# A decoder block: 1/rms applied behind the products in place of a normalised x, the second weight unit in quarters, ACT's table loaded by a first dummy square

## The chip, the cores and the metric

The kernel runs on one core of one Trainium2 chip. Its time is the device time of one execution in microseconds (us). Three runs of the kernel before gave 914.89, 915.78 and 917.61, median 915.78. A core has five engines with queues of their own, which meet only through semaphores: TensorE (PE, matrix products into PSUM), VectorE (DVE), ScalarE (ACT), GpSimd (POOL) and SyncE (SP, which here only starts DMA transfers). Each executes its instructions in the order in which they stand.

## The reference, cut to what matters

One block over 512 positions with 1024 channels, in float32:

```
h  = rmsnorm(x, g_mix);  z = h @ w_in            # a, gate | q, k | v | two gates
u  = a * sigmoid(gate)                           # GLU
yc = silu(layernorm(conv31(u))) @ w_conv_pw      # depthwise, causal, 31 taps
q, k = rope(q), rope(k);  o = diff_attention(q, k, v)       # 8 heads, two softmaxes each
ya = rmsnorm(o, g_subln) * 0.8 @ w_attn_pw
x  = x + (gate_conv * yc + gate_attn * ya) @ w_out
h2 = rmsnorm(x, g_ffn)
x  = x + (silu(h2 @ w_gate) * (h2 @ w_up)) @ w_down
out = rmsnorm(x, g_final)
```

with `rmsnorm(x, g) = x * rsqrt(mean(x*x) + eps) * g` over the channels. The first rmsnorm is what the change is about: a row's factor 1/rms can be multiplied to x ahead of `w_in` or to the products behind it.

## The kernel before

**Data.** Activations lie transposed, channels on the 128 partitions and the 512 positions along the free axis; x is eight tiles `xt[0..7]`. All weights are cut into units of 128 x 1024 (512 KB) that are used one after the other. Every fp32 factor is split into a high part in the matmul's type fp32r and a low part, the remainder, and a product takes three matmuls of 128x512 (hi by hi, hi by lo, lo by hi). Of a unit, ACT casts the high part (`wh`), and the low part (`wl`) is a subtraction: on DVE for units 0 to 2 and from 64 on, on POOL in two halves for the others (`emit_split`, line 322). `next_unit` (341) starts the loads and splits of later units each time one is taken.

**A chunk** (`chunkA`, 404) takes two units and makes two outputs of 128x512 in PSUM, 48 matmuls in all. With `kouter` both outputs advance together, otherwise the first is done ahead of the second inside each unit. Eight chunks make the inputs of the GLU (i = 0 to 7), then come project_v and the q and k chunks of eight heads, eight chunks of gates, four of w_attn_pw, w_conv_pw and w_out each, and the feed-forward part.

**Start.** Line 433 on loads x tiles and the first unit in quarters, turn by turn, then unit 1 in one piece. `xg` is `xt * g_mix`, split, but not yet divided by the rms. The first three GLU chunks work on `xg`; meanwhile `SumSq` (364) squares the eight tiles on ACT and adds them up on DVE. The task `norm_x` (554) takes over: column sums on PE (`rstd_cols`, 380), the power -1/2 on POOL (`rc`), four diagonal tiles `dg` on DVE, a product that spreads them over the partitions (`bcast_cols`, 390), and the copy `R`, which holds 1/rms of each position on every partition.

**Before, R was used twice.** The GLU outputs of chunks 0 to 2 were multiplied by R behind the products (`evac_glu`, 520): DVE `t = gate * R`, ACT sigmoid, POOL `t * R`, DVE `u = a * t`. In the meantime `renorm` (545) made the normalised x: eight times `xt * g_mix * R` on DVE, split into `hn`, casts on ACT and subtractions on DVE. From chunk 3 on (`SWITCH`) everything used `hn`.

**The order** is fixed when the program is built. A model of the engines' clocks (`Model`, with costs per operation) decides where the work of tasks such as `norm_x`, the softmaxes or `conv_norm` goes between the matmuls. The 31 taps of each channel's convolution (`conv_ops`, 500 on) are filler: DVE gets one whenever the model's DVE clock is behind its PE clock, or waits for something. The convolution's norm (`conv_norm`) can start only when all 8 x 31 taps are done.

**Tail** (1015 to 1034): for each quarter of the positions the sum, a square with accumulation, `ms` by a power on POOL, then `x2 * ms * g_final` on DVE, `x0 * ms` on ACT, and two transfers out.

Of the kernel before, what the change touches and what calls it, by code (L numbers as in the profile page):

```python
# [17 lines left out]
FILL = 0.1  # L18
NCH = 2
NAT = 3  # L20
SWITCH = 3
# [146 lines left out]
def build(nw):  # L168
# [26 lines left out]
    with tile.TileContext(nc) as tc, contextlib.ExitStack() as homes:  # L195
# [3 lines left out]
        with tc.tile_pool(name="cn", bufs=1) as cn, \  # L199
# [5 lines left out]
            def nm(s):  # L205
                uid[0] += 1
                return f"{s}_{uid[0]}"
# [210 lines left out]

            warm = tl("T6", F32R)
            V.memset(f32(warm), 0.0)  # L420
            cold = psum("cv")
            for i in range(10):
                mm(cold, warm[:, 0:P], warm, True, True)
# [11 lines left out]
            raw0 = home["wr"].tile([P, 1024], F32, name=nm("wr"), tag="wr", bufs=3)  # L435
            model.alloc("wr", 3, raw0)
            first = []
            for i in range(4):
                load_x(i)
                w = slice(i * 256, (i + 1) * 256)  # L440
                load(raw0[:, w], w_d[0, :, w])
            wst["dma"] = wst["split"] = 1
            for i in range(4, 6):
                load_x(i)
            emit_dma()
            for i in range(6, 8):
                load_x(i)
            emit_dma()
            lamv = tl("T5")[:, :4 * HD]
            pick = cn.tile([P, 64], F32R, name="pick")  # L450
# [9 lines left out]
            make_identity(nc, ident)  # L460
            load(vec, vec_d)
            ss = SumSq("T3", V)
            hi0 = home["wh"].tile([P, 1024], F32R, name=nm("wh"), tag="wh", bufs=4)
            model.alloc("wh", 4, hi0)
            lo0 = home["wl"].tile([P, 1024], F32R, name=nm("wl"), tag="wl", bufs=4)
            model.alloc("wl", 4, lo0)
            wq.append((hi0, lo0))
            for i in range(8):
                w = slice(i * 256, (i + 1) * 256)
                if i == 0:  # L470
                    V.tensor_copy(hi0[:, w], raw0[:, w])
                xg.append(split_scaled(xt[i], gmix[:, i:i + 1], "T5"))
                if i < 4:
                    if i:
                        S.copy(hi0[:, w], raw0[:, w])
                    V.tensor_tensor(out=lo0[:, w], in0=raw0[:, w], in1=f32(hi0)[:, w], op=ALU.subtract)
                if i == 5:
                    emit_split()
            for i in range(8):
                ss.add(xt[i])  # L480
                if i == 2:
# [5 lines left out]


            R = tl("T6")
            hn = []  # L490
            co = [None] * 8
            csum, done = [], []

# [26 lines left out]
            def evac_glu(i):  # L520
                def f(c, ps):
                    if c == 0:
                        glu["a"] = ps
                        return
                    room("T5", 1)
                    t = tl("T5")
                    u = tl("T2")
                    V.memset(u[:, 0:CW - 1], 0.0)
                    if i < SWITCH:
                        V.tensor_tensor(out=t, in0=ps, in1=R, op=ALU.mult)  # L530
                        S.activation(t, t, AF.Sigmoid)
                        G.tensor_tensor(out=t, in0=t, in1=R, op=ALU.mult)
                    else:
                        S.activation(t, ps, AF.Sigmoid)
                    V.tensor_tensor(out=u[:, CW - 1:CW - 1 + T], in0=glu["a"], in1=t, op=ALU.mult)
                    drop("T5")
                    pend.append([0.0, conv_ops(i, u)])
                return f
# [3 lines left out]
            def hold(c, ps):  # L542
                held.append((c, ps))

            def renorm():
                for i in range(8):
                    yield clk["dve"]
                    V.scalar_tensor_tensor(out=xt[i], in0=xt[i], scalar=gmix[:, i:i + 1], in1=R, op0=ALU.mult, op1=ALU.mult)
                    if i:
                        hn.append(split(xt[i - 1], "T1"))  # L550
                hn.append(split(xt[7], "T1"))
                drop("T4", 8)

            def norm_x():
                yield need(ss.acc) + 1.5
                rc = yield from rstd_cols(ss.acc, 1e-6, "at")
                drop("T3", 8)
                pb = yield from bcast_cols(rc, "at")
# [12 lines left out]
            def when_normed(c, ps):  # L571
                drain_tasks("norm_x")
                second(c, ps)
                if c == 1:
                    spawn(renorm())
# [154 lines left out]
            def project_v(vhl):  # L730
                units = [next_unit(), next_unit()]
                for half in range(2):
                    room("T4", 2)
                    ps = psum("mm")
                    vh, vl = tl("T4", F32R), tl("T4", F32R)
                    for tt in range(2):
                        t = 2 * half + tt
                        sl = slice(tt * 256, (tt + 1) * 256)
                        xs = slice(t * P, (t + 1) * P)
                        for k in range(8):  # L740
                            hi, lo = units[k // 4]
                            yield need(hi, lo, ps)
                            w = slice((k % 4) * 256, (k % 4) * 256 + 256)
                            mm(ps[:, sl], hn[k][0][:, xs], hi[:, w], k == 0, False)
                            mm(ps[:, sl], hn[k][0][:, xs], lo[:, w], False, False)
                            mm(ps[:, sl], hn[k][1][:, xs], hi[:, w], False, k == 7)
                    S.copy(vh, ps)
                    V.tensor_tensor(out=vl, in0=ps, in1=f32(vh), op=ALU.subtract)
                    vhl.append((vh, vl))

            for h in range(NH):
                if h % 2 == 0:
                    vhl = []
                    run(project_v(vhl))
                qk = []
                run(chunkA(hn, [psum("mm"), psum("mm")], lambda c, ps: qk.append(rope(ps))))
                spawn(softmaxes(h, qk))
                spawn(outputs(h, vhl))

# [3 lines left out]
            def evac_gate(i):  # L763
                gs = []
                gates.append(gs)

                def f(c, ps):
                    g = tl("T4")
# [95 lines left out]

            spawn(head_norm())
            for i in range(8):
                run(chunkA(hn, [psum("mm"), psum("mm")], evac_gate(i)))
            drain_tasks("head_norm")
            spawn(conv_norm())

# [115 lines left out]
            for n in range(2):  # L986
# [24 lines left out]
                for t in range(4):  # L1011
# [50 lines left out]
```

## Time and profile before

| | |
|---|---|
| median of the runs | 915.78 us (914.89 to 917.61) |
| the profiled execution | 912.36 us, its span 910.6 us |
| PE | 882.8 us busy, 97%, 4246 matmuls |
| DVE | 573.1 us busy, 63%, 952 instructions |
| ACT | 373.7 us busy, 41% |
| POOL | 264.1 us busy, 29% |
| weights and x by queue q1 | 82.52 MB |

All times in rows are microseconds from the span's start. A row of a timeline gives the start, the duration, the engine, the operation and its tiles; in brackets stands how long the engine had stood idle before, and what ended that. Rows of like instructions that follow each other are put together with a count, so that their duration goes from the first one's start to the last one's end. Neighbours on one engine overlap a little (an instruction starts before the one ahead has written its last), so that distances between starts say more than durations. Since a helper records every operation, nearly all have the same line, and the names of tiles tell them apart: `mm`, `at` and `cv` are PSUM banks, `T` any of the large SBUF tiles, `wr`, `wh`, `wl` a weight unit raw, high and low.

### The profile page before, as it was taken

How to read it: one execution, taken by the hardware profiler on the slowest of the kernel's cores; microseconds unless marked ns; L12 is line 12 of the kernel's file. 1: busy time of each engine (PE TensorE's matmuls, PEld its weight loads, DVE VectorE, ACT ScalarE, POOL GpSimd, SP SyncE). 2: the span in 40 equal slices, each digit the busy share in tenths (PEclk: the TensorE clock that was granted, in tenths of full speed). 3: DMA queues.
4: the chain of work that ended last, by engine and by line, in shares of the span. 5: the costliest groups of instructions: out<-in, count | busy, mean ns of one | idle time of the engine just before them, and what ended most of it. 6: DMA issues, size and time to landing. Idle time of an engine off the chain costs nothing.

```text
span 910.6 us, 11126 instructions
## 1 busy us (share of the span) xinstructions
PE 882.8 (97%) x4246; PEld 730.8 (80%) x4246; DVE 573.1 (63%) x952; ACT 373.7 (41%) x615; POOL 264.1 (29%) x215
## 2 busy tenths in 40 slices
PE   8989999989998999999999999999999999999996
PEld 5768888878886777687888888888888888888886
DVE  6699999898989999957455563343343443422422
ACT  6332336655756874445322343322222222312212
POOL 2654566564736345454100001111111111000000
PEclk9999999999999999999999999999999999999999
DMA  8222222121211222222323441223333222332302
GB/s 278 93 87 100 92 90 74 64 77 47 93 47 46 70 73 72 76 102 92 100 73 133 153 148 51 90 94 107 103 109 98 93 93 92 116 99 87 116 24 93
DMA packets 26150, 85.20 MB, mean 94 GB/s; under 512 B 3040, under 2 KB 3808, under 8 KB 26096
## 3 DMA queue, kind: packets, MB, share of 16 engines
q1 hardware_dynamic: 24944, 82.52, 27.3%
q10 hardware_dynamic: 1152, 1.97, 0.6%
q8 instruction: 33, 0.54, 0.2%
q14 instruction: 21, 0.17, 0.1%
HBM read 82.38 MB, written 2.10 MB: 93 GB/s over the span
## 4 chain that ended last, share of the span: by engine, by line
PE 52%; DVE 0%; issue 0%; POOL 0%; ACT 0%; POOLq 0%
PE mm L141 27%; PE at L141 22%; PE cv L141 4%; DVE dg L141 0%; DVE T L141 0%; POOL rc L141 0%; ACT T L141 0%; POOLq L195 0%; POOL sm L141 0%; DVE fs L141 0%
## 5 line engine op out<-in xcount | busy, mean ns | idle before, releaser
L141 PE MATMUL mm<-T,wh 128*128 128x512 f32 x1360 | 424.9, 393 | 4.4 <-DVE T L141 3.5
L141 PEld LDWEIGHTS mm<-T,wh 128*128 128x128 f32 x1360 | 250.3, 188 | 58.2 <-DVE T L141 4.2
L141 PE MATMUL mm<-T,wl 128*128 128x512 f32 x680 | 265.6, 391 | 0.5 <-DVE wl L141 0.5
L141 POOL TENSOR_TENSOR wl<-wr,wh 128x512 fp32r<-128x512 f32 x122 | 165.9, 1385 | 174.8 <-ACT wh L141 167.5
L141 ACT CAST wh<-wr 128x1024 fp32r<-128x1024 f32 (+1 forms) x148 | 148.7, 1033 | 79.3 <-PE mm L141 38.7
L141 DVE SCALAR_TENSOR_TENSOR cv<-T,vec_sb,cv 128x512 f32<-128x512 f32 x232 | 160.5, 746 | 0.1
L141 POOL TENSOR_TENSOR T<-T,T 128x512 f32<-128x512 f32 x64 | 84.2, 1320 | 242.1 <-DVE T L141 220.7
L141 PE MATMUL at<-T,wh 128*128 128x512 f32 x496 | 154.3, 392 | 0.0
L141 PEld LDWEIGHTS mm<-T,wl 128*128 128x128 f32 x680 | 127.7, 188 | 28.4 <-DVE wl L141 1.0
L141 DVE TENSOR_TENSOR wl<-wr,wh 128x1024 fp32r<-128x1024 f32 (+1 forms) x88 | 101.9, 1186 | 69.7 <-ACT wh L141 69.3
L141 DVE TENSOR_TENSOR T<-T,T 128x512 fp32r<-128x512 f32 (+2 forms) x111 | 88.4, 798 | 58.3 <-ACT T L141 56.1
L141 ACT CAST T<-T 128x512 fp32r<-128x512 f32 (+2 forms) x112 | 67.6, 618 | 135.5 <-POOL T L141 82.2
L141 PEld LDWEIGHTS at<-T,wh 128*128 128x128 f32 x496 | 93.6, 189 | 19.5
L141 DVE TENSOR_TENSOR T<-mm,T 128x512 f32<-128x512 f32 (+1 forms) x76 | 51.7, 682 | 84.9 <-PE mm L141 77.3
L141 PE MATMUL mm<-wh,T 128*128 128x256 f32 (+1 forms) x432 | 100.5, 317 | 0.0
L141 PE MATMUL at<-T,wl 128*128 128x512 f32 x248 | 97.0, 391 | 0.0
L141 ACT ACTIVATE T<-T 128x512 f32<-128x512 f32 (+1 forms) x66 | 40.4, 621 | 123.8 <-DVE T L141 123.7
L141 DVE TENSOR_TENSOR T<-at,T 128x512 f32<-128x512 f32 (+4 forms) x59 | 38.0, 649 | 67.1 <-PE at L141 56.0
L141 ACT ACTIVATE T<-T,sm 128x128 f32<-128x128 f32 (+3 forms) x100 | 56.1, 562 | 58.5 <-DVE sm L141 55.1
L141 PEld LDWEIGHTS mm<-wh,T 128*128 128x128 f32 x432 | 73.0, 190 | 5.4
L141 PE MATMUL mm<-wl,T 128*128 128x256 f32 (+1 forms) x216 | 68.2, 316 | 0.0
L141 PEld LDWEIGHTS at<-T,wl 128*128 128x128 f32 x248 | 46.9, 189 | 9.8
(88 smaller groups left out, 651.9 us busy)
## 6 DMA issues: line engine op xcount, KB each, us to landing
wr<-wall SPq DMA_DIRECT2D x145, 512.0 KB, 3.3
T<-xT SPq DMA_DIRECT2D x16, 256.0 KB, 4.8
out<-T ACTq DMA_DIRECT2D x4, 256.0 KB, 2.8
out<-T SPq DMA_DIRECT2D x4, 256.0 KB, 2.6
wr<-wall SPq DMA_DIRECT2D x4, 128.0 KB, 4.4
T<-cs ACTq DMA_DIRECT2D x2, 256.0 KB, 4.6
T<-gfin SPq DMA_DIRECT2D x2, 256.0 KB, 4.6
T<-mask ACTq DMA_DIRECT2D x1, 256.0 KB, 5.0
```

What stands on the lines that cost most here:

```text
L141: r = f(*args, **kw)
```

## The change

- `xg` is kept for all of `w_in`; `renorm`, `hn` and `SWITCH` are gone, and with them the `kouter` order of chunk 3.
- R enters behind the products: in all eight GLU chunks, in the two rope tables `cs` (once, behind chunk 3), in the gates (a DVE product ahead of each sigmoid), and for v, where positions lie on partitions, by the column factors `rc`, in halves of 256 columns on ACT and DVE.
- Unit 1 is loaded and split in quarters as unit 0 is, beside x4 to x7; unit 2's split stands behind that loop, unit 3's where unit 2's was, behind the third square.
- A square of one column of the zeroed `warm` tile is ACT's first instruction, so that its table is loaded then.
- In the tail `x2 * g_final` comes ahead of the factor `ms`, and for the last quarter half of `x0 * ms` goes from ACT to DVE.

```diff
@@ start
             V.memset(f32(warm), 0.0)
+            S.activation(small(), f32(warm)[:, 0:1], AF.Square)
...
-            for i in range(4):
+            for i in range(8):
                 load_x(i)
-                w = slice(i * 256, (i + 1) * 256)
-                load(raw0[:, w], w_d[0, :, w])
-            wst["dma"] = wst["split"] = 1
-            for i in range(4, 6):
-                load_x(i)
-            emit_dma()
-            for i in range(6, 8):
-                load_x(i)
+                w = slice(i % 4 * 256, i % 4 * 256 + 256)
+                load(raws[i // 4][:, w], w_d[i // 4, :, w])
+            wst["dma"] = wst["split"] = 2
             emit_dma()
...
-                xg.append(split_scaled(xt[i], gmix[:, i:i + 1], "T5"))
-                if i < 4:
-                    if i:
-                        S.copy(hi0[:, w], raw0[:, w])
-                    V.tensor_tensor(out=lo0[:, w], in0=raw0[:, w], in1=f32(hi0)[:, w], op=ALU.subtract)
-                if i == 5:
-                    emit_split()
+                    V.tensor_copy(hi[:, w], raw[:, w])
+                xg.append(split_scaled(xt[i], gmix[:, i:i + 1], "T1"))
+                if i:
+                    S.copy(hi[:, w], raw[:, w])
+                V.tensor_tensor(out=lo[:, w], in0=raw[:, w], in1=f32(hi)[:, w], op=ALU.subtract)
+            emit_split()
             for i in range(8):
                 ss.add(xt[i])
                 if i == 2:
                     emit_split()
@@ evac_glu
-                    if i < SWITCH:
-                        V.tensor_tensor(out=t, in0=ps, in1=R, op=ALU.mult)
-                        S.activation(t, t, AF.Sigmoid)
-                        G.tensor_tensor(out=t, in0=t, in1=R, op=ALU.mult)
-                    else:
-                        S.activation(t, ps, AF.Sigmoid)
+                    V.tensor_tensor(out=t, in0=ps, in1=R, op=ALU.mult)
+                    S.activation(t, t, AF.Sigmoid)
+                    G.tensor_tensor(out=t, in0=t, in1=R, op=ALU.mult)
@@ renorm
-            def renorm():
-                for i in range(8):
-                    yield clk["dve"]
-                    V.scalar_tensor_tensor(out=xt[i], in0=xt[i], scalar=gmix[:, i:i + 1], in1=R, op0=ALU.mult, op1=ALU.mult)
-                    if i:
-                        hn.append(split(xt[i - 1], "T1"))
-                hn.append(split(xt[7], "T1"))
-                drop("T4", 8)
@@ GLU chunks
             for i in range(2, 8):
-                if i == SWITCH:
-                    drop("T5", 16)
-                    drain_tasks("renorm")
-                run(chunkA(xg if i < SWITCH else hn, [psum("mm"), psum("mm")], evac_glu(i), i == SWITCH))
+                run(chunkA(xg, [psum("mm"), psum("mm")], evac_glu(i)))
+                if i == 3:
+                    for a in range(2):
+                        V.tensor_tensor(out=cs[a], in0=cs[a], in1=R, op=ALU.mult)
@@ project_v
-                    S.copy(vh, ps)
-                    V.tensor_tensor(out=vl, in0=ps, in1=f32(vh), op=ALU.subtract)
+                    for tt in range(2):
+                        sl = slice(tt * 256, (tt + 1) * 256)
+                        r = rcol[0][:, 2 * half + tt:2 * half + tt + 1]
+                        S.mul(vh[:, sl], ps[:, sl], mul=r)
+                        V.scalar_tensor_tensor(out=vl[:, sl], in0=ps[:, sl], scalar=r, in1=f32(vh)[:, sl],
+                                               op0=ALU.mult, op1=ALU.subtract)
@@ evac_gate
-                    S.activation(g, ps, AF.Sigmoid, bias=vcol((C_BGC, C_BGA)[c], i))
+                    V.tensor_tensor(out=g, in0=ps, in1=R, op=ALU.mult)
+                    S.activation(g, g, AF.Sigmoid, bias=vcol((C_BGC, C_BGA)[c], i))
@@ tail
-                        V.scalar_tensor_tensor(out=x2, in0=x2, scalar=ms, in1=gf[1], op0=ALU.mult, op1=ALU.mult)
-                        S.mul(x0, x0, mul=ms)
+                        V.tensor_tensor(out=x2, in0=x2, in1=gf[1], op=ALU.mult)
+                        V.tensor_scalar(out=x2, in0=x2, scalar1=ms, scalar2=None, op0=ALU.mult)
+                        h0 = 256 if t == 3 else 512
+                        S.mul(x0[:, :h0], x0[:, :h0], mul=ms)
+                        if t == 3:
+                            V.tensor_scalar(out=x0[:, h0:], in0=x0[:, h0:], scalar1=ms, scalar2=None, op0=ALU.mult)
```

How the order moves is seen at three places. First ACT, from unit 0's last quarter to the squares, before (T_14 and T_15 are x6 and x7, T_38 on the squares, wh_167, wh_201 and wh_221 units 0, 1 and 2):

```order
L141 CAST wh_167<-wr_116 128x256
L141 ACTIVATE T_28_193<-T_11_129,gmix 128x512
L141 ACTIVATE T_30_197<-T_12_131,gmix 128x512
L141 CAST wh_201<-wr_133 128x1024
L141 ACTIVATE T_34_205<-T_14_135,gmix 128x512
L141 ACTIVATE T_36_209<-T_15_137,gmix 128x512
L141 ACTIVATE T_38_213<-T_7_117 128x512
L141 ACTIVATE T_39_215<-T_8_120 128x512
L141 ACTIVATE T_40_218<-T_9_123 128x512
L141 CAST wh_221<-wr_139 128x1024
L141 ACTIVATE T_43_225<-T_10_126 128x512
```

And after, from x6 on (T_15 and T_16 are x6 and x7, wh_174, wh_224 and wh_238 units 1, 2 and 3):

```order
L140 ACTIVATE T_35_212<-T_15_138,gmix 128x512
L140 CAST wh_174<-wr_119 128x256
L140 ACTIVATE T_37_218<-T_16_141,gmix 128x512
L140 CAST wh_174<-wr_119 128x256
L140 CAST wh_224<-wr_144 128x1024
L140 ACTIVATE T_41_228<-T_9_120 128x512
L140 ACTIVATE T_42_230<-T_10_123 128x512
L140 ACTIVATE T_43_233<-T_11_126 128x512
L140 CAST wh_238<-wr_236 128x1024
L140 ACTIVATE T_47_243<-T_12_129 128x512
L140 ACTIVATE T_48_246<-T_13_132 128x512
```

Unit 2's cast moved ahead of all squares, and unit 3's, which stood behind the eighth square, is now behind the third.

Second DVE, ahead of the product of the gate of chunk 2 with R (mm_412 times T_48), before (cv_406 is chunk 0's convolution, T_7 on are x0 on):

```order
L141 TENSOR_TENSOR T_74_400<-at_307,T_48_244 128x512
L141 TENSOR_SCALAR cv_406<-T_73_376,vec_sb 128x512
L141 SCALAR_TENSOR_TENSOR cv_406<-T_73_376,vec_sb,cv_406 128x512 x2
L141 TENSOR_TENSOR T_75_401<-mm_306,T_74_400 128x512
L141 SCALAR_TENSOR_TENSOR T_7_117<-T_7_117,gmix,T_48_244 128x512
L141 SCALAR_TENSOR_TENSOR T_8_120<-T_8_120,gmix,T_48_244 128x512
L141 TENSOR_TENSOR T_83_442<-T_7_117,T_82_440 128x512
...
L141 TENSOR_TENSOR T_94_496<-T_11_129,T_93_494 128x512
L141 MEMSET T_96_502 128x30
L141 TENSOR_TENSOR T_95_501<-mm_412,T_48_244 128x512
```

And after, the same products (mm_423 times T_52), as far as u of chunk 2 (cv_417 and cv_446 are the convolutions of chunks 0 and 1):

```order
L140 TENSOR_TENSOR T_75_411<-at_318,T_52_262 128x512
L140 TENSOR_SCALAR cv_417<-T_74_390,vec_sb 128x512
L140 SCALAR_TENSOR_TENSOR cv_417<-T_74_390,vec_sb,cv_417 128x512 x2
L140 TENSOR_TENSOR T_76_412<-mm_317,T_75_411 128x512
L140 TENSOR_SCALAR cv_446<-T_76_412,vec_sb 128x512
...
L140 SCALAR_TENSOR_TENSOR cv_417<-T_74_390,vec_sb,cv_417 128x512
L140 MEMSET T_88_498 128x30
L140 TENSOR_TENSOR T_87_497<-mm_423,T_52_262 128x512
L140 SCALAR_TENSOR_TENSOR cv_446<-T_76_412,vec_sb,cv_446 128x512
L140 SCALAR_TENSOR_TENSOR cv_417<-T_74_390,vec_sb,cv_417 128x512
L140 SCALAR_TENSOR_TENSOR cv_446<-T_76_412,vec_sb,cv_446 128x512
L140 TENSOR_TENSOR T_88_498<-mm_422,T_87_497 128x512
```

The renormalisation's rows are gone; taps stand in their place, and three of them between the two products of a chunk.

Third DVE behind chunk 3, after (T_1 and T_2 are the rope tables, mm_508 and mm_507 the two outputs of chunk 3):

```order
L140 TENSOR_TENSOR T_97_583<-mm_508,T_52_262 128x512
L140 SCALAR_TENSOR_TENSOR cv_417<-T_74_390,vec_sb,cv_417 128x512
L140 SCALAR_TENSOR_TENSOR cv_446<-T_76_412,vec_sb,cv_446 128x512
L140 SCALAR_TENSOR_TENSOR cv_417<-T_74_390,vec_sb,cv_417 128x512
L140 TENSOR_TENSOR T_98_584<-mm_507,T_97_583 128x512
L140 TENSOR_TENSOR T_1_98<-T_1_98,T_52_262 128x512
L140 TENSOR_TENSOR T_2_99<-T_2_99,T_52_262 128x512
```

The products with R and with the tables are new there; before, a chunk from 3 on had one product and fourteen taps.

## Rows read from the trace of the kernel before

**Rows 1.** The page, busy time and share of the span by engine, instructions.

```profile
PE 882.8 (97%) x4246; PEld 730.8 (80%) x4246; DVE 573.1 (63%) x952; ACT 373.7 (41%) x615; POOL 264.1 (29%) x215
```

**Rows 2.** Timeline of PE: start, duration, operation, count, idle before and releaser.

```profile
24.03 1.02 PE L141 MATMUL at<-ones,T 128*128 128x1 f32 x8 [2.40 <-DVE T L141]
...
36.37 0.61 PE L141 MATMUL mm<-T,wh 128*128 128x512 f32 x2
...
37.05 0.61 PE L141 MATMUL mm<-T,wh 128*128 128x512 f32 x2
...
51.27 0.74 PE L141 MATMUL mm<-T,wh 128*128 128x512 f32 x2 [3.18 <-DVE T L141]
```

**Rows 3.** Busy time of PE, PEld, DVE, ACT, POOL by stretch; granted clock, DMA.

```profile
25.00:29.00 4.00, 4.00 (x12) 3.14 (x12) 1.89 (x3) 0.00 (x0) 4.00 (x5) 0.57 0.65 230
...
134.00:345.00 211.00, 199.74 (x1132) 168.99 (x1130) 192.92 (x430) 142.88 (x303) 116.66 (x87) 1.00 0.20 68
345.00:425.00 80.00, 79.18 (x340) 59.63 (x341) 63.88 (x97) 33.83 (x48) 41.48 (x28) 1.00 0.26 86
```

**Rows 4.** Timeline of PE at the convolution's norm.

```profile
415.19 1.05 PE L141 MATMUL at<-ones,T 128*128 128x1 f32 x8
...
421.56 0.94 PE L141 MATMUL cv<-dg,ones 128*128 128x128 f32 x6 [0.73 <-DVE dg L141]
```

**Rows 5.** Timeline of DVE, the two products with R.

```profile
36.57 0.69 DVE L141 TENSOR_TENSOR T<-at,T 128x512 f32<-128x512 f32 x1 [0.80 <-PE at L141]
...
50.56 0.65 DVE L141 TENSOR_TENSOR T<-mm,T 128x512 f32<-128x512 f32 x1
```

**Rows 6.** Timeline of ACT, a quarter's cast, five squares, unit 3's cast.

```profile
9.59 0.39 ACT L141 CAST wh<-wr 128x256 fp32r<-128x256 f32 x1
...
16.63 2.71 ACT L141 ACTIVATE T<-T 128x512 f32<-128x512 f32 x5
19.25 1.03 ACT L141 CAST wh<-wr 128x1024 fp32r<-128x1024 f32 x1
```

**Rows 7.** Timeline of POOL, unit 3's lo halves, the power, a product with R.

```profile
20.36 2.97 POOL L141 TENSOR_TENSOR wl<-wr,wh 128x512 fp32r<-128x512 f32 x2 [16.12 <-ACT wh L141]
...
26.20 1.03 POOL L141 TENSOR_TENSOR rc<-sm,mhalf 128x4 f32<-128x4 f32 x1
...
51.96 1.30 POOL L141 TENSOR_TENSOR T<-T,T 128x512 f32<-128x512 f32 x1 [5.70 <-ACT T L141]
```

**Rows 8.** Timeline of DVE, adds of the sum of squares.

```profile
18.02 0.68 DVE L141 TENSOR_TENSOR T<-T,T 128x512 f32<-128x512 f32 x1
...
20.40 1.80 DVE L141 TENSOR_TENSOR T<-T,T 128x512 f32<-128x512 f32 x1
...
22.31 1.57 DVE L141 TENSOR_TENSOR T<-T,T 128x512 f32<-128x512 f32 x1
```

**Rows 9.** Timeline of DVE, one GLU chunk, from product to product.

```profile
65.78 0.67 DVE L141 TENSOR_TENSOR T<-mm,T 128x512 f32<-128x512 f32 x1
66.37 9.32 DVE L141 SCALAR_TENSOR_TENSOR cv<-T,vec_sb,cv 128x512 f32<-128x512 f32 x14
...
75.61 0.67 DVE L141 TENSOR_TENSOR T<-mm,T 128x512 f32<-128x512 f32 x1
```

**Rows 10.** PE's waits from 134 to 345: total us, times, longest.

```profile
PE at L141 <- DVE T L141: 5.1, 10, 0.9
PE at L141 <- DVE kz L141: 3.6, 5, 1.3
```

**Rows 11.** Timeline, a scaling of 512 columns, and the tail.

```profile
401.06 0.43 DVE L141 TENSOR_SCALAR T<-T 128x512 f32<-128x512 f32 x1 [7.23 <-POOL T L141]
...
904.99 0.55 POOL L141 TENSOR_TENSOR sm<-fs,mhalf 128x1 f32<-128x1 f32 x1 [3.29 <-DVE fs L141]
...
905.57 0.75 DVE L141 SCALAR_TENSOR_TENSOR T<-T,sm,T 128x512 f32<-128x512 f32 x1 [0.66 <-POOL sm L141]
906.32 0.37 ACTq L1034 DMA_DIRECT2D out<-T  x1
```

More of the change, by code (lines that the diff above doesn't have):

```diff
@@ L20 @@
 NAT = 3
-SWITCH = 3
 C_GMIX, C_BGC, C_BGA, C_BDW, C_GLN, C_BLN, C_GFFN, C_GSUB, C_WDW = 0, 8, 16, 24, 32, 40, 48, 56, 57
@@ L434, in build @@
             load(gmix, vec_d[:, C_GMIX:C_GMIX + 8])
-            raw0 = home["wr"].tile([P, 1024], F32, name=nm("wr"), tag="wr", bufs=3)
-            model.alloc("wr", 3, raw0)
+            raws, his, los = [], [], []
+            for _ in range(2):
+                raws.append(home["wr"].tile([P, 1024], F32, name=nm("wr"), tag="wr", bufs=3))
+                model.alloc("wr", 3, raws[-1])
             first = []
-            for i in range(4):
+            for i in range(8):
                 load_x(i)
-                w = slice(i * 256, (i + 1) * 256)
-                load(raw0[:, w], w_d[0, :, w])
-            wst["dma"] = wst["split"] = 1
-            for i in range(4, 6):
-                load_x(i)
-            emit_dma()
-            for i in range(6, 8):
-                load_x(i)
+                w = slice(i % 4 * 256, i % 4 * 256 + 256)
+                load(raws[i // 4][:, w], w_d[i // 4, :, w])
+            wst["dma"] = wst["split"] = 2
             emit_dma()
@@ L462, in build @@
             ss = SumSq("T3", V)
[L463 to L467, printed above, removed]
+            for _ in range(2):
+                his.append(home["wh"].tile([P, 1024], F32R, name=nm("wh"), tag="wh", bufs=4))
+                model.alloc("wh", 4, his[-1])
+                los.append(home["wl"].tile([P, 1024], F32R, name=nm("wl"), tag="wl", bufs=4))
+                model.alloc("wl", 4, los[-1])
+                wq.append((his[-1], los[-1]))
             for i in range(8):
-                w = slice(i * 256, (i + 1) * 256)
+                w = slice(i % 4 * 256, i % 4 * 256 + 256)
+                raw, hi, lo = raws[i // 4], his[i // 4], los[i // 4]
                 if i == 0:
-                    V.tensor_copy(hi0[:, w], raw0[:, w])
-                xg.append(split_scaled(xt[i], gmix[:, i:i + 1], "T5"))
-                if i < 4:
-                    if i:
-                        S.copy(hi0[:, w], raw0[:, w])
-                    V.tensor_tensor(out=lo0[:, w], in0=raw0[:, w], in1=f32(hi0)[:, w], op=ALU.subtract)
-                if i == 5:
-                    emit_split()
+                    V.tensor_copy(hi[:, w], raw[:, w])
[4 more added lines that the diff above has]
+            emit_split()
             for i in range(8):
@@ L489, in build @@
             R = tl("T6")
-            hn = []
+            rcol = []
             co = [None] * 8
@@ L557, in norm_x @@
                 drop("T3", 8)
+                drop("T4", 8)
+                rcol.append(rc)
                 pb = yield from bcast_cols(rc, "at")
@@ L573, in when_normed @@
                 second(c, ps)
-                if c == 1:
-                    spawn(renorm())
             run(chunkA(xg, [psum("mm"), psum("at")], when_normed))
             for i in range(2, 8):
-                if i == SWITCH:
-                    drop("T5", 16)
-                    drain_tasks("renorm")
-                run(chunkA(xg if i < SWITCH else hn, [psum("mm"), psum("mm")], evac_glu(i), i == SWITCH))
+                run(chunkA(xg, [psum("mm"), psum("mm")], evac_glu(i)))
+                if i == 3:
+                    for a in range(2):
+                        V.tensor_tensor(out=cs[a], in0=cs[a], in1=R, op=ALU.mult)
             lp = small(2 * HD, "lp", 1)
@@ L743, in project_v @@
                             w = slice((k % 4) * 256, (k % 4) * 256 + 256)
-                            mm(ps[:, sl], hn[k][0][:, xs], hi[:, w], k == 0, False)
-                            mm(ps[:, sl], hn[k][0][:, xs], lo[:, w], False, False)
-                            mm(ps[:, sl], hn[k][1][:, xs], hi[:, w], False, k == 7)
-                    S.copy(vh, ps)
-                    V.tensor_tensor(out=vl, in0=ps, in1=f32(vh), op=ALU.subtract)
+                            mm(ps[:, sl], xg[k][0][:, xs], hi[:, w], k == 0, False)
+                            mm(ps[:, sl], xg[k][0][:, xs], lo[:, w], False, False)
+                            mm(ps[:, sl], xg[k][1][:, xs], hi[:, w], False, k == 7)
+                    for tt in range(2):
[4 more added lines that the diff above has]
+                                               op0=ALU.mult, op1=ALU.subtract)
                     vhl.append((vh, vl))
@@ L755, in build @@
                 qk = []
-                run(chunkA(hn, [psum("mm"), psum("mm")], lambda c, ps: qk.append(rope(ps))))
+                run(chunkA(xg, [psum("mm"), psum("mm")], lambda c, ps: qk.append(rope(ps))))
                 spawn(softmaxes(h, qk))
@@ L767, in f @@
                 def f(c, ps):
+                    room("T4", 1)
                     g = tl("T4")
-                    S.activation(g, ps, AF.Sigmoid, bias=vcol((C_BGC, C_BGA)[c], i))
+                    V.tensor_tensor(out=g, in0=ps, in1=R, op=ALU.mult)
+                    S.activation(g, g, AF.Sigmoid, bias=vcol((C_BGC, C_BGA)[c], i))
                     gs.append(g)
@@ L866, in build @@
             for i in range(8):
-                run(chunkA(hn, [psum("mm"), psum("mm")], evac_gate(i)))
+                run(chunkA(xg, [psum("mm"), psum("mm")], evac_gate(i)))
             drain_tasks("head_norm")
```

## The prediction

> **What bounds the kernel now.** I read the busy shares first, then busy time by stretch, then the timelines of the five engines where TensorE (PE) stands still, and last PE's waits. PE is busy 882.8 us of the span of 910.6 [rows 1]; 27.8 us are idle, and only these can be won, since the count of matmuls stays. They lie at the column sums of the norm (2.40 before 24.03 [rows 2]), at the third GLU chunk (3.18 before 51.27 [rows 2]), in the attention stretch (211 less 199.74, 11.3 us [rows 3]), before the convolution's norm (0.73 at 421.56 [rows 4]); the rest, by subtraction some 10 us, is the start and the tail. Three matmuls start 0.68 us after the three before (36.37 to 37.05 [rows 2]), so a chunk of 48 takes 16 x 0.68 = 10.88 us. The reader is to see that the two waits on DVE (VectorE) early on are of different kinds: the first is a chain that has to run (squares, adds, sums, power, broadcast), the second is a queue, for DVE renormalises x and reaches g2 x R only at 50.56 [rows 5].
>
> **Start, as far as the second chunk's end.** The table load leaves the way of x0, and unit 1 comes in quarters, so the first chunk ends some 2 us earlier; but PE then stands before the column sums, whose time the sum of squares sets. ACT (ScalarE) has four casts of a quarter, 0.39 each, in place of one whole one of 1.0 [rows 6]: +0.56. The cast of unit 3, in before behind the last five squares at 19.25, now stands ahead of them: +1.0. So those squares run from 16.63 + 1.56 = 18.2 to 20.9, and POOL (GpSimd) starts the two lo halves of unit 3 at 18.3, not at 20.36 [rows 7]. That is what costs: an add of the sum of squares takes 0.68 us alone, and 1.80 and 1.57 while POOL has a half [rows 8]. In before two adds met halves; now five do. The first ends at about 20.05 (the half of 18.3 has to end, then 0.6 for the add), the others follow each 1.75 later (the mean distance of the ends of rows 8 is 1.68 to 1.9), one less if it slips in between POOL's two units at 21.4 to 22: the sum is complete at about 26.2, the column sums C start at 26.3 instead of 24.03. From C to the end of chunk 1 it was 36.37 - 24.03 = 12.34 [rows 2]. Now rc need not wait for POOL (C's sums end at 25.05, rc starts at 26.20 [rows 7], with POOL free some 0.2 later: -0.9), and 21 matmuls are left behind the broadcast instead of 24 (-0.68): 10.76, so chunk 1 ends at 37.06: **+0.7**. Ends of the range: all adds slip between the halves, C stays at 24.0: -1.6; none does, C = 27.2: +1.6. I stay with the alternating pattern, since rows 8 show it twice running.
>
> **The renormalisation goes.** Eight scaled products and eight lo subtractions leave DVE, eight casts ACT, and chunk 3 no longer needs hn. g2 x R follows the taps; from 36.57 to the same place DVE now has the chain of g1 (2.73, below), a product (0.60) and ten taps of 0.659 [rows 9]: 9.9 us, against 10.88 of PE. So it comes at chunk 2's end, and chunk 3's second bank is wanted only 12 matmuls (2.72) later. The 3.18 go: **-3.2** (at worst -2.5).
>
> **What is late next: the GLU chunks.** Each chunk from 3 on gets ps x R on DVE and t x R on POOL. From the start of g2 x R (50.56) over the sigmoid to POOL's product (51.96 + 1.30 [rows 7]) the chain takes 2.73 before DVE may multiply by a; three taps fill it. Then DVE has that product and twelve more taps. From 65.78 to 75.61 one product and 14 taps took 9.83 [rows 9]: 0.60 and 14 x 0.659. A chunk of after is 2.73 + 0.60 + 12 x 0.659 = 11.24, so DVE loses 0.36 on PE in each. In chunk 3's turn the two table products cs x R stand in for two taps; both read SBUF twice and run while POOL makes halves, so by rows 8 they take 1.57 to 1.80, together some 1.5 more than two taps. DVE may be 2.0 late before PE waits (2.72 less 0.67 and the hand-over). It stands at 0.2 after chunk 2, 0.6 after 3, 2.5 after 4: half a microsecond of waiting, and 0.36 at each of the two next: **+1.1**. Nothing if the table products meet no half and the lag starts at 0; +2.5 if POOL's product is late by a half each time. Project_v follows. To the first q that is, as an estimate, 96 matmuls of half the columns and 36 whole ones, 19 us of PE, and on DVE a last chain, its product, 18 taps and four products of 256 columns (some 0.4): 2.73 + 0.60 + 11.9 + 1.6 = 16.8. That pays the lag back.
>
> **Attention, gates, convolution's norm.** Order and work in attention are nearly those of before; its DVE waits (5.1 and 3.6 [rows 10]) may move either way: **0**, from -1.5 to +1.5. The gates get 16 products of 0.67 on DVE, two a chunk, 1.34 on 10.88; DVE there is busy 63.88 of 80 [rows 3], so they are covered; were the cover gone, each would hold up a bank 2.7 us after its chunk. The convolution's taps end later, and between the norm's column sums and the broadcast PE has 12 matmuls instead of 18. That chain takes from 415.19 to 421.56 [rows 4], and 6 x 0.227 = 1.4 of its cover goes; against it, rc there waited for POOL's halves too. **+0.8**, the ends being -0.7 (no half in the way: the present 0.73 go) and +2.0 (the whole cover lost, another 0.6 for a later DVE).
>
> **Tail.** x2 x gf is done ahead of ms, then a scaling; for the last tile half of x0's scaling goes to DVE. A scaling of 512 columns takes 0.43 [rows 11], one of 256 some 0.25. With ms at 905.57 as before, DVE is done with both at 906.2, against 906.32 for the last transfer of before [rows 11]: -0.1. But the product can start a tenth ahead of POOL's power (904.99 [rows 11]): if they get in each other's way as add and half do in rows 8, the power comes 0.5 later: +0.5. **+0.2**, nearer to rows 8. The Trainium skill ("SBUF — State Buffer", section "SBUF: two separate sides") says that a DVE operation with two SBUF inputs and a GpSimd one take the shared ports in turn, whichever starts first holding them for its whole instruction; rows 8 agree with that (1.80 against 0.68), a power beside a product no row shows. By that rule the tail is +0.5, without it -0.1.
>
> **Sum**: 0.7 - 3.2 + 1.1 + 0 + 0.8 + 0.2 = -0.4 us. Against the profiled execution (912.36) that is 911.96. That execution lies 3.4 under the median of the runs, 915.78, so the forecast is put on the median: **915.4**.
>
> **Rivals.**
> 1. *The start and DVE come out well.* The adds slip between the halves (-1.6), the lag stays under 2.0 (+0.3 left), the norm's chain is freed of POOL (0), tail -0.1: -4.6, **911.2**. For it: an add that meets no half takes 0.68 [rows 8], and POOL has a gap between its two units. Against it: POOL starts 2 us earlier, and its queue then is nearly full.
> 2. *DVE becomes the bound in attention (slower).* PE waits 15 times for DVE there, 8.7 us [rows 10]; DVE is busy 192.92 of 211 [rows 3]. If the lag of some 2 us from the GLU chunks isn't paid back in project_v, and taps shifted behind it stand ahead of softmax work, each wait grows by about 0.25: 3.8 more, **919.2**. It decides from the point at which DVE is still late at the first q. Against it: the 2 us of room in project_v.
> 3. *The clock.* After the wait of 2.40 the granted clock was 0.57 in 25 to 29 [rows 3], the lower of its two levels, 1.2 GHz, in most of it; the twelve or so matmuls there lay beside the chain to the broadcast and cost nothing. PE will wait about 5.5 us this time (from some 20.8, by the earlier first chunk, to 26.3). If the low clock lasts past the broadcast, 21 matmuls at twice 0.227 cost 4.7 more: **920.1**. Against it: after 3.18 at 51.27 the matmuls of rows 2 run on at once. The Trainium skill ("TensorE: Matmul & The Clock Gate", section "Part 1: The HAM clock gate") has an idle engine fall to the lower clock and return only after it has been busy for a while, which speaks for this rival; the row of 25 to 29 agrees, the one of 51.27 shows a pause without it.
> 4. *The wait at 51.27 only moves.* If R is 3 us later still, DVE enters chunk 2 late and g2 x R comes no sooner: -0.4 + 3.2, **918.6**. Against it: 0.9 us of room in chunk 2.
>
> **Chances.** The forecast 0.45 (its own range 913.0 to 917.9), rival 1 0.27, rival 2 0.14, rival 3 0.07, rival 4 0.07. Two executions of this kernel differ by about 0.3% (2.75 us). Faster than 913.0: most of rival 1 (0.24) and the low end of the forecast (0.06), 0.30. Slower than 918.5: rivals 2 and 3 mostly (0.15), half of 4 and the forecast's high end (0.05), 0.20. The rest 0.50. The range cuts off the low end of rival 1 and the upper halves of 2 and 3: 910.8 to 919.3.
>
> **What would show it.** On DVE, adds of 1.6 to 1.9 between 18 and 26 and column sums at 26.3: the first term; column sums before 25 make it rival 1. PE with no wait at chunk 3's second bank, and one of 0.3 to 0.7 on DVE T in each of chunks 5 to 7: terms two and three; no wait there, or waits from chunk 4 on, would show the lag missized. A wait of 1.3 to 1.6 <- DVE dg before the convolution's broadcast. In the tail, a power that begins only when DVE's product ends. The forecast is wrong in kind if PE's idle time in attention leaves 10 to 13 us.

## Result and the profile after

The changed kernel takes 922.53 us (922.01 to 923.73) against 915.07 for the kernel before, both medians of 5 runs: 1.0084 times as long, 95% interval 1.0072 to 1.0096. The forecast was 915.4, no change, in a range of 910.8 to 919.3. The change is slower by 7.5 us.

The page after, its first lines; the row of engines answers to [rows 1]:

```profile
span 920.7 us, 11176 instructions
## 1 busy us (share of the span) xinstructions
PE 888.6 (97%) x4246; PEld 733.6 (80%) x4246; DVE 587.6 (64%) x975; ACT 372.1 (40%) x619; POOL 270.4 (29%) x220
```

The count of PE's matmuls is the same, so the traces can be laid side by side by number: when did the n-th matmul start? Worked out from the traces, in us (chunk 2 begins with matmul 122, chunk 3 with 170):

| n | what lies ahead | before | after | difference |
|---|---|---|---|---|
| 120 | start, norm, most of chunk 1 | 35.91 | 38.97 | +3.06 |
| 200 | chunk 2, start of chunk 3 | 57.52 | 57.10 | -0.42 |
| 412 | the other GLU chunks | 105.35 | 106.62 | +1.27 |
| 520 | v, first q chunk | 119.83 | 121.10 | +1.27 |
| 1720 | attention, first gates | 346.63 | 356.44 | +9.81 |
| 2120 | gates, convolution's norm | 440.27 | 449.97 | +9.70 |
| 4245 | all the rest | 903.43 | 913.25 | +9.82 |

The two profiled executions lie 10.1 us apart, the medians 7.5: the profiled execution of before (912.36) lies under all five of its timed runs, and the section on the hardware says where it may have gained.

At the start, timeline of PE after (start, duration, operation, idle before and releaser); the last row is chunk 2's beginning, where [rows 2] have 36.37:

```profile
27.09 1.84 PE L140 MATMUL at<-ones,T 128*128 128x1 f32 x8 [5.94 <-DVE T L140]
...
33.73 1.05 PE L140 MATMUL at<-dg,ones 128*128 128x128 f32 x8
...
39.42 0.62 PE L140 MATMUL mm<-T,wh 128*128 128x512 f32 x2
```

The column sums wait 5.94 us where they waited 2.40. DVE's adds and POOL's halves beside them, after, one row each for runs of like operations:

```profile
19.60 7.34 DVE L140 TENSOR_TENSOR T<-T,T 128x512 f32<-128x512 f32 x5 [0.42 <-ACT T L140]
```

```profile
19.12 2.97 POOL L140 TENSOR_TENSOR wl<-wr,wh 128x512 fp32r<-128x512 f32 x2 [14.88 <-ACT wh L140]
22.66 2.93 POOL L140 TENSOR_TENSOR wl<-wr,wh 128x512 fp32r<-128x512 f32 x2 [0.57 <-ACT wh L140]
```

Five adds take 7.34. One by one, four of them meet a half and take 1.36 to 1.72, and the last one, behind the halves, takes 0.69; alone they take 0.68 [rows 8].

PE's waits from 134 to 350 (waited for, total us, times, longest), after; the same window before has 5.7, 3.6, 0.6 and 1.1:

```profile
PE at L140 <- DVE T L140: 9.4, 13, 1.4
PE at L140 <- DVE kz L140: 3.2, 5, 1.3
PE at L140 <- DVE sm L140: 1.6, 5, 0.4
PE at L140 <- ACT T L140: 1.0, 2, 0.8
```

In attention, between matmuls 520 and 1720, lie 8.5 us of the loss, and the forecast had put nothing there. The rows of this stretch, first after, then before, and last the part of it in which the clock falls, after (length, busy times of PE, PEld, DVE, ACT and POOL, granted clock, DMA):

```profile
121.10:356.44 235.34, 219.31 (x1201) 183.15 (x1200) 213.18 (x459) 147.62 (x312) 128.31 (x96) 0.99 0.21 69
119.83:346.63 226.80, 215.53 (x1201) 181.86 (x1200) 208.26 (x454) 147.35 (x309) 128.25 (x95) 1.00 0.21 69
241.00:245.00 4.00, 3.99 (x13) 3.32 (x14) 3.02 (x14) 1.91 (x8) 0.84 (x1) 0.57 0.39 133
```

- PE's idle time, the length less PE's busy time, goes from 11.3 to 16.0, which is 4.8 of the 8.5.
- A wait costs more than its row shows, since the matmuls behind it start late by some 0.3 more: in the GLU chunks a wait of 0.34 at 75.29 comes with a delay of 0.66 between matmuls 272 and 284. After has 26 waits of over 0.15 in the stretch and before 20; as an estimate that is 1.8.
- The clock falls once, after, to its lower level in most of 241 to 245; before it stays at 1.00. What that costs is seen in the run e8 below: at matmul 1427 it has the same wait as before (1.26), its clock falls behind it (0.66 from 289 to 294) and before's doesn't, and from matmul 1420 to 1470 it loses 1.5 on before.

The three together make some 8 of the 8.5.

By place, three make 7.7 of the 8.5: after loses 1.8 on before between matmuls 820 and 920, 5.0 between 1070 and 1170, and 0.9 between 1370 and 1470. The first and the third are alike, a cluster of waits. The first, PE after and then before:

```profile
180.74 0.88 PE L140 MATMUL at<-ident,T 128*128 128x128 f32 x6 [1.32 <-DVE T L140]
...
184.47 0.33 PE L140 MATMUL at<-kz,T 128*128 128x128 f32 x1 [0.72 <-DVE kz L140]
187.62 0.33 PE L140 MATMUL at<-T,T 128*128 128x128 f32 x1 [1.38 <-DVE T L140]
...
189.72 0.39 PE L140 MATMUL at<-T,T 128*128 128x256 f32 x1 [0.42 <-DVE sm L140]
```

```profile
176.33 0.88 PE L141 MATMUL at<-ident,T 128*128 128x128 f32 x6 [0.68 <-DVE T L141]
...
182.57 0.33 PE L141 MATMUL at<-kz,T 128*128 128x128 f32 x1 [0.41 <-DVE kz L141]
...
184.97 0.33 PE L141 MATMUL at<-kz,T 128*128 128x128 f32 x1 [1.26 <-DVE kz L141]
...
193.28 0.44 PE L141 MATMUL at<-ident,T 128*128 128x128 f32 x2 [0.57 <-DVE T L141]
```

Four waits, 3.84 us together; the cluster comes again at 286.40 to 295.39. Before has waits at both places too, 2.92 here and 3.19 at 274.40 to 291.94, so that only the surplus is lost. The second place is the costliest: before has no wait over 0.15 there, after has 3.13 in four, and the fall of the clock comes right behind them. PE after:

```profile
231.27 0.88 PE L140 MATMUL at<-ident,T 128*128 128x128 f32 x6 [0.67 <-DVE T L140]
...
237.50 0.33 PE L140 MATMUL at<-kz,T 128*128 128x128 f32 x1 [0.32 <-DVE kz L140]
...
239.43 0.30 PE L140 MATMUL at<-T,T 128*128 128x128 f32 x1 [0.86 <-DVE T L140]
...
241.01 0.33 PE L140 MATMUL at<-kz,T 128*128 128x128 f32 x1 [1.28 <-DVE kz L140]
```

What DVE does ahead of these waits, after, three operations at the first place and two at the second:

```profile
178.92 1.76 DVE L140 SCALAR_TENSOR_TENSOR T<-T,sm,T 128x512 f32<-128x512 f32 x1 [0.19 <-ACT T L140]
180.71 1.67 DVE L140 TENSOR_TENSOR T<-T,T 64x512 fp32r<-64x512 f32 x1
...
185.17 1.67 DVE L140 TENSOR_TENSOR kz<-T,T 64x512 fp32r<-64x512 f32 x1
...
237.47 1.81 DVE L140 TENSOR_TENSOR T<-T,T 64x512 fp32r<-64x512 f32 x1
239.31 1.64 DVE L140 TENSOR_TENSOR kz<-T,T 64x512 fp32r<-64x512 f32 x1
```

All five read SBUF twice; such operations take some 0.7 alone (0.68 to 0.75 in e9 below). POOL beside them, after:

```profile
178.86 2.97 POOL L140 TENSOR_TENSOR wl<-wr,wh 128x512 fp32r<-128x512 f32 x2
184.64 3.32 POOL L140 TENSOR_TENSOR wl<-wr,wh 128x512 fp32r<-128x512 f32 x2 [2.81 <-ACT wh L140]
...
237.45 2.95 POOL L140 TENSOR_TENSOR wl<-wr,wh 128x512 fp32r<-128x512 f32 x2 [2.59 <-ACT wh L140]
```

Each of the five lies beside a pair of halves.

### The profile page after: what moved, and what is told of

Its sections match the earlier page's. It is cut to its first block, busy times and chain, and to the rows that moved or that the text cites. A ratio compares the mean times of both kernels' runs of the same rounds, so it can differ in the third digit from the quotient of the medians.

```text
span 920.7 us, 11176 instructions
## 1 busy us (share of the span) xinstructions
PE 888.6 (97%) x4246; PEld 733.6 (80%) x4246; DVE 587.6 (64%) x975; ACT 372.1 (40%) x619; POOL 270.4 (29%) x220
## 4 chain that ended last, share of the span: by engine, by line
PE 68%; DVE 16%; ACT 5%; issue 4%; POOL 4%; DMA 1%; SPq 0%; POOLq 0%; ACTq 0%; DVEq 0%
PE mm L140 39%; PE at L140 25%; DVE T L140 10%; ACT T L140 4%; PE cv L140 4%; DVE cv L140 4%; POOL wl L140 3%; DVE kz L140 1%; POOL T L140 1%; DMA wr<-wall 1%; ACT wh L140 1%; DMA T<-xT 1%; ACT L140 0%; SPq L232 0%; DVE sm L140 0%
## 5 line engine op out<-in xcount | busy, mean ns | idle before, releaser
L140 POOL TENSOR_TENSOR T<-T,T 128x512 f32<-128x512 f32 x69 | 90.3, 1311 | 288.1 <-DVE T L140 237.2
L140 DVE TENSOR_TENSOR T<-T,T 128x512 f32<-128x512 f32 (+2 forms) x109 | 92.2, 848 | 58.8 <-ACT T L140 57.1
L140 DVE TENSOR_TENSOR T<-mm,T 128x512 f32<-128x512 f32 (+1 forms) x89 | 60.6, 682 | 85.1 <-PE mm L140 79.6
L140 ACT ACTIVATE T<-T 128x512 f32<-128x512 f32 (+1 forms) x71 | 43.4, 622 | 176.2 <-DVE T L140 176.2
L140 ACT CAST T<-T 128x512 fp32r<-128x512 f32 (+2 forms) x104 | 62.7, 618 | 126.9 <-POOL T L140 82.4
```

The source lines that it names most:

```text
L140: r = f(*args, **kw)
```

## The experiments

Each was timed beside the kernel before on the same chip (medians of before 913.91 to 915.10); ratios are to it. Cuts of code are shortened. "Attention" is the time between the starts of matmuls 520 and 1720, "GLU" between 200 and 412, "C" the start of the column sums.

**v's eviction as it was (e1).**

```diff
-   for tt in range(2): S.mul(vh[:, sl], ps[:, sl], mul=r); V.scalar_tensor_tensor(out=vl[:, sl], ...)
+   S.copy(vh, ps)
+   V.tensor_tensor(out=vl, in0=ps, in1=f32(vh), op=ALU.subtract)
```

> The changed kernel with v's eviction as it was before: one ACT copy and one DVE subtraction of 512 columns. It leaves out the factor 1/rms of v, so only its time counts. Theory 1 (order): the 8.5 us lost in the attention stretch come from another order of instructions there, which the planner chose because v's eviction is four DVE and ACT operations of other costs; with the old eviction the order is nearly the old one, the stretch from matmul 520 to 1720 goes from 235.4 back to 226 to 228 us, time 914 to 915.5. Theory 2 (DVE's load): the loss comes from DVE being late out of the GLU chunks and having more work; both stay, the stretch stays at 233 to 236, time 921 to 923.

912.18, ratio 0.9977 (0.9968 to 0.9986); attention 225.67, both a little under theory 1's ranges. Ten us for an edit of two instructions per half: theory 1.

**The kernel before with v in halves (e2).** `S.copy` and `V.tensor_tensor` twice over 256 columns.

> The kernel before with v's eviction cut in halves of 256 columns, and nothing else; the same values. Theory 1 (order): the attention order becomes nearly that of the changed kernel, the stretch goes from 226.8 to 233 to 236 us, time 921 to 924. Theory 2 (DVE's load): only four operations of 256 columns take the place of two of 512, 0.2 us more on DVE each time, hidden; time 915 to 916.

923.94, ratio 1.0112 (1.0092 to 1.0133); attention 234.98. Of the 8.5 us 8.2 appear in the old kernel with nothing else of the change: theory 1.

**Unit 3 split late (e3).** In the loop of squares:

```diff
-                if i == 2:
-                    emit_split()
```

> The changed kernel without the split of unit 3 behind the third square; it comes behind the eighth, as in the kernel before. Theory 1 (POOL holds the adds): the adds run in 0.7 us, the column sums start at 22 to 23 instead of 27.1, PE stands 1 to 2 us there and not 5.9, the clock falls less; chunk 1 ends at 34 to 36 instead of 39.4; time 917 to 919. Theory 2 (the squares come late anyway, for ACT's casts of quarters): column sums at 25 or later, time 920.5 or more.

919.76, ratio 1.0065 (1.005 to 1.008), 2.8 under the changed kernel; C at 23.78, attention unchanged at 235.34. This lies between the two theories' ranges, nearer to the first: the halves did hold the adds, but the last add still met the first half, and the clock fell no less (0.57 from 23 to 31; in the changed kernel 0.62 from 25 to 34):

```profile
17.29 6.35 DVE L140 TENSOR_TENSOR T<-T,T 128x512 f32<-128x512 f32 x7
```

**v in halves, the planner told it is whole (e4).** The same engine instructions as in the changed kernel, called past the planner, and two costs entered by hand:

```diff
+   model.op("act", 0.04 + 512 * 0.0009, [p], [a])
+   model.op("dve", 0.065 + 512 * 0.00104, [p, a], [b])
```

> The changed kernel with all its work, v in halves and scaled; only the planner is told the cost of one copy and one subtraction of 512 columns. Theory 1 (order): attention's order is that of the run with v whole, the stretch takes 226 to 229 us, time 914 to 916. Theory 2 (DVE's load): 921 to 923. If v whole is fast and this one slow, the four operations themselves are the cost.

916.01, ratio 1.0011 (0.9997 to 1.0025); attention 227.77. Theory 1: the same work in the other order is 6.5 us faster by the medians and 7.6 in the attention stretch of the traces. The 2 us over e1's attention are the price of the work itself, or of e1's slightly other timing; the runs do not part these.

**The kernel before, the planner told v comes in halves (e8).** The reverse: instructions as before, two costs of 256 columns each.

> The kernel before with all its operations as they were; only the planner is told that v's copy and subtraction are two of 256 columns each. Theory 1 (order alone): the attention stretch takes 233 to 236 us as with v in halves, time 921 to 924. Theory 2 (the cut operations cost something on the engines): 226 to 228, 914 to 916.

920.80, ratio 1.0068 (1.0055 to 1.008); attention 234.21. Theory 1: no instruction was added, only the order changed, and 7.4 of the 8.5 us appear. Two falls of the clock are in them, 0.66 each from 238 to 243 and from 289 to 294; the second cost 1.5, so the two make 3 as an estimate. The cluster is there, PE of this run:

```profile
180.44 0.87 PE L141 MATMUL at<-ident,T 128*128 128x128 f32 x6 [1.35 <-DVE T L141]
...
184.17 0.33 PE L141 MATMUL at<-kz,T 128*128 128x128 f32 x1 [0.74 <-DVE kz L141]
187.31 0.33 PE L141 MATMUL at<-T,T 128*128 128x128 f32 x1 [1.37 <-DVE T L141]
189.42 0.39 PE L141 MATMUL at<-T,T 128*128 128x256 f32 x1 [0.42 <-DVE sm L141]
```

**Why that order is bad (e9, e10).** In both kernels ACT makes the low half in the attention stretch, as a plain copy, and POOL's halves of units 16 to 39 fall away:

```diff
+   if 16 <= i < 40: nc.scalar.copy(lo, raw)
+   ...  model.op("pool", 0.05 + 512 * 0.0023, ...)   # in place of G.tensor_tensor
```

> The changed kernel in its own order, but in the attention stretch (units 16 to 39) the low half of a weight unit is a copy of the raw unit by ACT, and POOL does none of its 48 subtractions there; that leaves out the subtraction. The planner is told POOL's cost as before. Theory 1 (the bad order is bad because DVE's operations with two SBUF inputs meet POOL's halves at places where PE waits): the waits near 180 to 190 and 286 to 296 mostly go, the stretch goes from 235.3 to 226 to 229. Theory 2 (the order is bad by itself, too few matmuls beside each chain): it stays at 232 to 236.

> The kernel before in its own order with the same edit. Theory 1: its stretch has fewer such meetings where PE waits and gains less, 226.8 to 222 to 225, so the distance to the changed kernel falls from 8.5 to under 4. Theory 2: 224 to 227, and the distance stays at 7 or more.

e9 took 918.14 (ratio 1.0043, 1.0028 to 1.0058), attention 231.49, 3.8 less; e10 913.68 (0.9995, 0.9982 to 1.0008), attention 227.80, no less (some 1.4 of it a fall of the clock, 0.66 from 284 to 289, that before doesn't have). The distance fell from 8.5 to 3.7, or to 5.1 without that fall: neither theory's number, between the two. But e9 holds its own control. Its first cluster and the place behind it lie where POOL has no halves, its second cluster where units from 40 on are being split and POOL has them again. PE of e9, all three places in order of time:

```profile
179.64 0.87 PE L140 MATMUL at<-ident,T 128*128 128x128 f32 x6 [0.34 <-DVE T L140]
184.56 0.33 PE L140 MATMUL at<-T,T 128*128 128x128 f32 x1 [0.37 <-DVE T L140]
186.67 0.39 PE L140 MATMUL at<-T,T 128*128 128x256 f32 x1 [0.44 <-DVE sm L140]
...
229.79 0.87 PE L140 MATMUL at<-ident,T 128*128 128x128 f32 x6 [0.74 <-DVE T L140]
237.02 0.33 PE L140 MATMUL at<-kz,T 128*128 128x128 f32 x1 [0.30 <-DVE kz L140]
...
281.40 0.87 PE L140 MATMUL at<-ident,T 128*128 128x128 f32 x6 [1.34 <-DVE T L140]
285.12 0.33 PE L140 MATMUL at<-kz,T 128*128 128x128 f32 x1 [0.70 <-DVE kz L140]
288.27 0.33 PE L140 MATMUL at<-T,T 128*128 128x128 f32 x1 [1.38 <-DVE T L140]
290.38 0.39 PE L140 MATMUL at<-T,T 128*128 128x256 f32 x1 [0.43 <-DVE sm L140]
```

In the first cluster 1.15 us of waits, against 3.85 in the second; at the place between them 1.04, where the changed kernel has 3.13, and the clock stays at 1.00. In the first, DVE's combining product takes 0.75 and not 1.76:

```profile
178.84 0.75 DVE L140 SCALAR_TENSOR_TENSOR T<-T,sm,T 128x512 f32<-128x512 f32 x1 [0.19 <-ACT T L140]
179.62 0.68 DVE L140 TENSOR_TENSOR T<-T,T 64x512 fp32r<-64x512 f32 x1
```

At the place between, DVE's two operations take 0.69 each and not 1.81 and 1.64. So most of the waits at these two places are made of POOL's halves. Against before, e9 gains 1.1 at the first place and loses 1.6 and 0.8 at the others, where the changed kernel lost 1.8, 5.0 and 0.9; between e9 and e10 the first two places differ by 2.1, between the changed kernel and before by 6.8. Elsewhere e9 loses 2.5 more than the changed kernel, with ACT, which makes the copies, busy for 166.91 of the stretch instead of 147.62. What the rest of the distance between the two orders is made of stays open.

**Repairs together (e5).** e4 and e3 and the old tail.

> The changed kernel with three edits: v costed as whole for the planner, unit 3 split behind all squares, the tail as it was before. If the three losses are independent, they add: from 916.0 (v costed as whole) 2.8 for the start (column sums at 23.8, as with unit 3 late alone) and 0.4 for the tail (from the last fs to the last transfer 1.6 instead of 2.0): 912.8, attention stretch 227.8. If the start's gain is given back where DVE is late in the GLU chunks, 914.5 or more.

911.48, ratio 0.9962 (0.9948 to 0.9975): faster than both, and 1.3 under the 912.8 expected, so that the three losses add up, and a little more. C 23.82, GLU 49.52, attention 227.84. The tail, from the last fs to the last transfer's issue, takes 1.56 (903.53 to 905.09); in the changed kernel it takes 2.03:

```profile
914.69 0.16 DVE L140 SCALAR_TENSOR_TENSOR fs<-fs,fs 128x1 f32<-128x1 f32 x1 [0.57 <-ACT T L140]
914.76 0.69 DVE L140 TENSOR_TENSOR T<-T,T 128x512 f32<-128x512 f32 x1
914.93 0.92 POOL L140 TENSOR_TENSOR sm<-fs,mhalf 128x1 f32<-128x1 f32 x1 [3.03 <-DVE fs L140]
...
916.72 0.34 ACTq L1030 DMA_DIRECT2D out<-T  x1
```

POOL's power takes 0.92 beside the product and 0.55 without [rows 11].

**Rope tables on POOL (e6), and unit 3's low part on DVE (e7).** `V.tensor_tensor(out=cs[a], ...)` becomes `G.tensor_tensor`; then `if i < 3` in the split becomes `if i < 4`.

> The combined kernel with the two products of the rope tables with 1/rms on POOL instead of DVE. Theory 1 (they make DVE late, because they wait for POOL's halves): the GLU stretch from matmul 200 to 412 goes from 49.5 to 48.1 to 48.4, PE's waits for DVE in chunks 5 to 7 shrink to under 0.4 in all; 911.4. Theory 2 (DVE's 11.24 a chunk alone make the waits): 49.2 to 49.5, no change.

> The same, and unit 3's low part on DVE behind the adds instead of on POOL. Theory 1 (POOL's half still holds the last adds): column sums at 22 to 22.6 instead of 23.8, chunk 1 ends 1 to 2 earlier; 909.5 to 910.5. Theory 2 (the squares on ACT set the end of the sum): column sums at 23.3 or later, no change.

e6: 912.23 (0.9974, 0.996 to 0.9987), GLU 48.04, a little better than theory 1 has it, and attention 229.54, 1.7 more than e5's, which took the gain back; e11 shows how much of that is the order. e7: 912.40 (0.9967, 0.9953 to 0.998); C at 23.38, as theory 2 has it: all seven adds take 0.69 and start 0.79 apart, at the pace of the squares; and two waits on dg, 1.67 and 0.73, appear ahead of the broadcast. Nothing gained.

**The tables on POOL, the order kept (e11).** As in e4: the instruction on POOL, DVE's cost entered by hand.

> The combined kernel with the rope tables' two products on POOL, and the planner told DVE's cost, so that PE, ACT and the rest of DVE keep the order of the combined kernel. Theory 1 (the tables make DVE late in the GLU chunks, and where they stood on POOL without gain, attention's order had changed): GLU stretch 48.1, attention 227 to 228.5, time 1.0 to 1.6 under the combined kernel's 911.5, so 910. Theory 2 (the attention stretch grows because DVE comes out of the GLU chunks earlier or POOL later): attention 229 or more, 911.5 to 912.5.

910.29, ratio 0.9946 (0.9934 to 0.9959), the lowest median of all. GLU 47.83, no wait of PE for DVE between 40 and 120, attention 228.54. That is theory 1 for the GLU chunks and the time; but the interval overlaps that of e5, so the 1.2 us between the two medians are not shown by the times alone. Attention is 1.0 under e6's, which the order may explain, and still 0.7 over e5's.

## Why the prediction was wrong

**The step that failed** is "Order and work in attention are nearly those of before; its DVE waits may move either way: 0". It cost 8.5 us in the traces, more than five times the end of its own range, and e8 shows that the order alone makes 7.4 of it. The prediction's own sign for an error in kind, PE's idle time in attention outside 10 to 13 us, came true with 16.0. An order nearly that of before was taken for one that costs the same. In a stretch where PE waits for DVE 15 times and DVE is nine tenths busy, small moves decide which of DVE's operations meet a half on POOL; e9 shows this for the two costliest places. The price of a fall of the clock in attention was in no term and no rival.

**Rival 2** named attention and a loss, 3.8, but by another mechanism, and that one is refuted: DVE's lag was paid back, as the 1.27 at matmuls 412 and 520 shows and 200 more matmuls in which the two traces stay in step, and e4 keeps the GLU lag (49.52) and loses only 1.0 in attention. Rivals 1 and 4 are refuted as well: C came at 27.09 and not before 25, and the wait at chunk 3 went.

**Start, +0.7, measured +3.06.** The mechanism was right: adds and halves alternate (four adds met one, not five), C at 27.09, forecast 26.3 with 27.2 as the end. Mis-sized was C to the end of chunk 1, 10.76 forecast, 12.33 measured: the clock was at its lower level behind the long pause, the eight column sums took 1.84 instead of 1.02, and twelve matmuls ran until 33.73. Rival 3 had the clock, but past the broadcast it was full again (0.98 from 33 to 40). Part of the +3.06 is chance: e1, e4 and e9, which have the same instructions as far as here, end chunk 1 at 38.02, 38.03 and 38.27 and not at 39.42, which is +1.7 to +1.9.

**Chunk 3, -3.2, measured -3.48**: right. The wait of 3.18 is gone, and with it the 0.3 by which a wait delays the starts behind it.

**GLU, +1.1, measured +1.69**: right in kind. The two table products took 2.86 together, and one wait for DVE came in each of chunks 5 to 7, as forecast (0.34, 0.07 and 0.34 idle, each with a delay of 0.36 to 0.66); e6 and e11 take 1.5 to 1.7 away by moving these products alone.

**Convolution's norm, +0.8, measured -0.1.** With 12 matmuls instead of 18 beside it the chain was 1.4 shorter (428.99 to 433.96, against 6.37 in [rows 4]), since the power did not wait for halves (it starts 0.24 behind the operation that feeds it, and 1.62 before); the wait is 0.73 in both.

**Tail, +0.2, measured +0.3 to +0.5**: the power and the product get in each other's way. The Trainium skill ("SBUF — State Buffer", section "SBUF: two separate sides") has a GpSimd operation blocked by a DVE operation with two SBUF inputs that started first. 0.92 against 0.55 agrees in kind: the product started first, at 914.76, and the power ended 0.40 after it.

## What to carry to other kernels

Where a planner sets the order, compare the order in every stretch in which an engine waits often, and price a change there by its spread, not at nothing; an edit of two small instructions moved some 8 us, about a hundred us further on. Compare starts and not idle times, since a wait costs more than its row shows. Time the arithmetic with the order held still (tell the planner the old cost) before judging the arithmetic. And ask of each piece of POOL work that moves which DVE operations with two SBUF inputs it will now meet.

## What was not expected of the hardware

In these traces the clock behind a pause of the same length is not the same each time. Ahead of chunk 3 the kernel before pauses 3.18 us; in its profiled execution the clock stayed at 1.00 behind it, in e8, with a start at 51.29 and a pause of 3.17, it was 0.65 from 51.3 to 56:

```profile
51.30:56.00 4.70, 4.70 (x14) 3.77 (x15) 4.68 (x8) 1.79 (x4) 1.28 (x1) 0.65 0.00 0
```

In e2 it was 0.50 and in e10 0.65. From matmul 120 to 200 these three took 23.09, 24.25 and 23.24, not 21.61. So in three of four traces the wait that the change removes cost 1.5 to 2.6 more than in the profile of before. That may account for most of the 2.6 us by which the distance of the profiles exceeds that of the medians; no trace of the other executions of before shows it. In the other place the pauses of 2.74 (e3) and 2.78 (e5) ahead of the column sums were followed by sums of 1.84 and 1.02. Between matmuls 520 and 1720 the clock fell once each in the changed kernel, e2 and e3 and twice in e8, all with the bad order or one like it; of the other nine traces only e5 and e10 have a fall there, one each. Whether the waits bring the falls about is not shown.
